# Block sums of the input spread over three feature tiles, and the first head's decay rows and context loaded before its query matrix

## The chip, the cores and the metric

One core of a Trainium2 chip runs the whole block. The metric is the device time of one execution, in microseconds (us). Engines are named as the profile names them: PE is TensorE's matmul, PEld its weight load, DVE is VectorE, ACT is ScalarE, POOL is GpSimd, and SP is SyncE, whose queue issues every DMA of this kernel.

## The reference

Two layers act on 1024 latent tokens of 1024 features, with a context of 256 tokens before them. Layer 0 mixes with a bidirectional mLSTM, layer 1 with box means over a grid of tokens. The part that matters here is layer 0:

```python
def mlstm_features(h, w_in, conv_w, conv_b, w_q, w_k, w_v):
    xm, z, og = jnp.split(h @ w_in, 3, axis=-1)
    xc = jax.nn.silu(short_conv(xm, conv_w, conv_b))
    q = headwise(xc, w_q)
    k = headwise(xc, w_k) * (MLSTM_HEAD_DIM ** -0.5)
    v = headwise(xm, w_v)
    return q, k, v, xc, z, og
...
        d = jnp.where(tril, b[..., :, None] - b[..., None, :] + ic[..., None, :], -jnp.inf)
        s = jnp.einsum("bhld,bhsd->bhls", qc, kc) * jnp.exp(d - m_t[..., None])
```

`h` is the input after RMSNorm and the shift and scale of the conditioning. `h @ w_in` gives three parts of 2048 columns: xm, z and og. The scores of a head are products of queries and keys, times decays exp(d).

## The kernel before

Every fp32 matmul is made of three: an operand is split into a rounded part and the rest (ACT casts, DVE subtracts), and hi·hi, hi·lo and lo·hi are summed in PSUM (`mm3`, line 136).

The stages, in order of time. **Start** (0 to 75 us): norms and the conditioning. **Feature tiles** (75 to about 395 us): 16 tiles of 128 columns of xm, `features(n)`, each in three chunks of 512, 512 and 256 tokens. ACT copies a chunk out of PSUM twice (L373 plain, L375 cast), DVE takes the rest of the split (L376). Then come the convolution (ACT L378, DVE L379 and L380, ACT SiLU L381), the split of its result (L388, L389) and the writes to DRAM. Between the matmuls of tile n+1, PE works through `token_part(n)`: ten small products (PSUM tag `pb`), each 128 tokens of tile n's cast xm against a small matrix; ACT copies each to SBUF (L415), and after five of them DVE adds (L416) and ACT casts (L418). `pb` has two buffers, so the product number s+2 needs the copy of product s. PE's order in this stage is written out by hand; each engine works strictly in the order of its own list.

**z and og columns** (to about 704 us): a seven-product block scheme (`strassen`) needs sums of blocks of h. Those are made by `block_sums()` during the feature tiles, four times (k = 0 to 3): load two rows of h from DRAM (L519), four DVE sums (L522 to L525), and for each of four results an ACT cast (L529), a DVE subtraction (L530) and a write to DRAM (L531). It is a generator, and the loop over tiles advances it by a number of `yield`s per tile, from tile 2 on.

**Heads** (704 to 1228 us): for each of four heads and eight query tiles, scores (`score_chunk`, chunks 0 and 1 of the latent tokens, chunk 2 of the context), decays (`decay`, ACT Exp of rows that are broadcast from DRAM, L769 to L773), their product (DVE L755), weights, transposes and values. Ahead of the first head stand the loads of its keys `xh_d`, `xl_d` (`fetch_x`: L692 latent, L686 context), of the decay rows (`load_gates` L713, `load_ctx_gates` L706), the matrix A (`make_A`) and the first queries (`make_q`: PE, ACT cast L735, DVE L736). In this stage a scheduler orders the instructions of every engine, each before the run and for good. **Rest**: output product, layer 1.

Large tiles share 32 buffers of 4 KB per partition (tag `S4`); `hn` has 3 buffers of 2 KB. In the block scheme's last tile all 32 are in use, and loads for the first head are issued as PE sets them free.

Of the kernel before, what the change touches and what calls it, by code (L numbers as in the profile page):

```python
# [17 lines left out]
P = 128  # L18
# [3 lines left out]
TC = 256  # L22
# [29 lines left out]
def hybrid_block(ctx: ExitStack, tc: tile.TileContext, xT, ctxT, vecs, w_ada0, w_ada, w_blk, w_krow, blk_mask, w_gate, w_in, b_gate, w_out,  # L52
# [10 lines left out]
    def nm(s):  # L63
        uid[0] += 1
        return f"{s}_{uid[0]}"
# [11 lines left out]
    def tl(tag, shape, dt=F32):  # L77
        n = int(np.prod(shape[1:])) * 4
        assert n <= BYTES[tag], (tag, shape)
        pool = ph["pool"] if tag in PHASED else sb  # L80
        return pool.tile(list(shape), dt, tag=tag, bufs=BUFS[tag], name=nm(tag))
# [3 lines left out]
    def pt_(tag, shape=(P, 512)):  # L85
        return ps.tile(list(shape), F32, tag=tag, bufs=PBUFS[tag], name=nm(tag))
# [4 lines left out]
    def f(t):  # L91
        return t.bitcast(F32)

    def const1(shape, name, dt=F32):
        return ph["pool"].tile(list(shape), dt, name=name)
# [157 lines left out]
    h = {}  # L253
# [94 lines left out]
    def bilinear():  # L348
        wkr = tl("S4", [P, KE, 4, 4])
        nc.sync.dma_start(wkr, w_krow)  # L350
        G.tensor_tensor(wkr, wkr, wb[:, 0, :, None, :].to_broadcast([P, KE, 4, 4]), op=ALU.mult)
        V.tensor_reduce(amat, wkr, axis=AX.X, op=ALU.add)
        V.tensor_scalar(amat, amat, QSCALE, None, op0=ALU.mult)
# [157 lines left out]
    def block_sums():  # L511


        dsh = const1([P, 4, 1], "dsh")
        V.tensor_tensor(dsh, mod0[:, 4:8, 0, 0:1], mod0[:, 0:4, 0, 0:1], op=ALU.subtract)
        for k in range(4):
            t0, t1 = tl("S4", [P, T]), tl("S4", [P, T])
            for t, kk in ((t0, k), (t1, k + 4)):
                nc.sync.dma_start(t, h_d[kk])  # L519
            yield  # L520
            b11, b12, b21, b22 = t0[:, :512], t0[:, 512:], t1[:, :512], t1[:, 512:]
            V.scalar_tensor_tensor(b22, b22, dsh[:, k], b12, op0=ALU.add, op1=ALU.subtract)  # L522
            V.tensor_tensor(b12, b12, b11, op=ALU.subtract)
            V.scalar_tensor_tensor(b11, b22, mod0[:, k, 0, 0:1], b11, op0=ALU.add, op1=ALU.add)
            V.scalar_tensor_tensor(b21, b21, mod0[:, k + 4, 0, 0:1], b11, op0=ALU.add, op1=ALU.subtract)  # L525
            yield
            for j, x in ((2, b11), (3, b22), (1, b12), (4, b21)):
                t = tl("S4", [P, 2, 512], F32R)
                S.activation(t[:, 0], x, AF.Copy)  # L529
                V.tensor_tensor(t[:, 1], x, f(t[:, 0]), op=ALU.subtract)  # L530
                nc.sync.dma_start(t_d[j - 1, k], f(t))  # L531
                yield

    side, parts, sums = iter(()), [], block_sums()
    with ctx0:
        gate_weights()
        for n in range(KE):
            out = features(n, side)
            for _ in side:
                pass  # L540
            if n == 1:
                gacc.extend(pt_("pc") for _ in range(3))
            if n == 2:
                bilinear()
            if n >= 2:
                for _ in range(3 if n < 10 else 2):
                    next(sums, None)
            parts.append(token_part(n, *out))
            if n:
                side = chain(*parts)  # L550
                parts = []
# [129 lines left out]
    def fetch_x(hd, h, ci):  # L681
        for part, src in (("xh", xh_d), ("xl", xl_d)):
            ts = hd.setdefault(part, {})
            if ci == 2:
                t = tl("S4", [P, 4, TC], F32R)
                nc.sync.dma_start(f(t), src[4 * h:4 * h + 4, :, T:TA].rearrange("c p t -> p c t"))  # L686
                for c in range(4):
                    ts[c, ci] = t[:, c]
                continue
            for c2 in range(2):  # L690
                t = tl("S4", [P, 2, 512], F32R)
                nc.sync.dma_start(f(t), src[4 * h + 2 * c2:4 * h + 2 * c2 + 2, :, 512 * ci:512 * ci + 512].rearrange("c p t -> p c t"))  # L692
                for j in range(2):
                    ts[2 * c2 + j, ci] = t[:, j]

    def fetch_v(hd, h, j0, j1):
        for j in range(j0, j1):
            for part, src in (("vh", vh_d), ("vl", vl_d)):
                t = tl("S4", [P, 2, DH], F32R)
                nc.sync.dma_start(f(t), src[h, :, 2 * j:2 * j + 2])  # L700
                hd.setdefault(part, []).append(t)

    def load_ctx_gates(h):
        rc = tl("hn", [P, 2, TC])
        for d in range(2):
            nc.sync.dma_start(rc[:, d], a_d[32 * d + h:32 * d + h + 1, T:TA].to_broadcast([P, TC]))  # L706
        return rc

    def load_gates(h):
        out = []  # L710
        for d in range(2):
            r = tl("S4", [P, T])
            nc.sync.dma_start(r, a_d[32 * d + h:32 * d + h + 1, 0:T].to_broadcast([P, T]))  # L713
            out.append(r)
        return out

    def make_A(h):
        ah, al = tl("wh", [P, 4, 32, 4], F32R), tl("wl", [P, 4, 32, 4], F32R)
        r = tl("wr", [P, 4, 32, 4])
        for c in range(4):  # L720
            V.tensor_tensor(r[:, c], mask, amat[:, 4 * h + c:4 * h + c + 1].to_broadcast([P, 32, 4]), op=ALU.mult)
        V.tensor_copy(ah, r)
        V.tensor_tensor(al, r, f(ah), op=ALU.subtract)
        return ah.rearrange("p c a b -> p c (a b)"), al.rearrange("p c a b -> p c (a b)")
# [113 lines left out]
    def start_head(h):  # L838
        hd = {}
        fetch_x(hd, h, 0)  # L840
        return dict(h=h, hd=hd)

    def next_q(cur, tp):
        return make_q(cur["hd"], cur["A"], tp)

    def finish_x(cur):
        for ci in (1, 2):
            fetch_x(cur["hd"], cur["h"], ci)

    cur = start_head(0)  # L850
    fetch_x(cur["hd"], 0, 1)
    cur["A"] = make_A(0)
    cur["q"] = next_q(cur, 0)
    cur["R"], cur["rc"] = load_gates(0), load_ctx_gates(0)
    fetch_x(cur["hd"], 0, 2)
    fetch_v(cur["hd"], 0, 0, 5)
    st_prev = st_now = nxt = None
    for i in range(len(seq) + 1):
        st = None
        if i < len(seq):  # L860
            h, ti = seq[i]
            more = h + 1 < NH
            st = dict(cur, ti=ti)
            decay(st)
            if ti == 7 and more:
                nxt["rc"], nxt["R"] = load_ctx_gates(h + 1), load_gates(h + 1)
            score_chunk(st, 0)
# [33 lines left out]
        if st and ti == 7:  # L901
            cur = nxt
# [385 lines left out]
```

## Time and profile before

| what | value |
|---|---|
| median of three runs | 2068.04 us (2063.6 to 2069.58) |
| profiled execution, its own time | 2062.41 us |
| its span | 2060.7 us |
| PE busy | 1982.7 us, 96% |
| DVE, ACT, POOL busy | 61%, 39%, 14% |
| mean granted clock of TensorE | 0.986 |
| HBM traffic | 164 GB/s over the span |

The span runs from the first to the last instruction of the profiled execution; its own time is 1.7 us longer. PE is busy nearly throughout: 78 us of the span have no matmul. The chain of waits is 86% PE.

### The profile page before, as it was taken

Reading aid. Unit: us, or ns where it says so; the run is one execution under the profiler, and the core shown is the slowest. Engines: PE = TensorE matmul, PEld = TensorE weight load, DVE = VectorE, ACT = ScalarE, POOL = GpSimd, SP = SyncE. Lnnn points to the kernel's source line nnn. Section 1 sums busy time; section 2 is a strip of 40 time slices with the busy share of each in tenths; the row PEclk is TensorE's granted clock in tenths of the full one; section 3 lists DMA queues with packets and bytes.
Section 4 is the critical chain, followed back from the end, with each engine's and each line's share of the span. In section 5 each row is a group of like instructions: output and inputs, shape, how many; then the busy total and the mean of one; then the engine's idle time right before and its main releaser. Section 6 shows DMA issues by size and latency. Waiting matters only on the chain.

```text
span 2060.7 us, 26787 instructions
## 1 busy us (share of the span) xinstructions
PE 1982.7 (96%) x10050; PEld 1668.4 (81%) x10050; DVE 1258.9 (61%) x2092; ACT 809.4 (39%) x1353; POOL 289.5 (14%) x376
## 2 busy tenths in 40 slices
PE   6888889999999999999999999999999999999997
PEld 4777778788888788888888878887888888888897
DVE  4766666787677667667576672544747283744444
ACT  5566666533333432333323322443423132224443
POOL 1000000023322100000000001343000000000275
PEclk9999999999999999999999999999999999999999
DMA  9376776864444854638346334534331312134573
GB/s 364 135 249 219 233 245 215 275 221 128 148 137 125 274 200 139 225 123 275 109 161 213 108 97 138 193 115 164 101 112 51 103 52 87 52 114 137 177 249 127
DMA packets 202499, 339.47 MB, mean 165 GB/s; under 512 B 13021, under 2 KB 116957, under 8 KB 202369
## 3 DMA queue, kind: packets, MB, share of 16 engines
q1 hardware_dynamic: 202368, 337.76, 48.8%
q8 instruction: 78, 1.28, 0.2%
q14 instruction: 53, 0.43, 0.1%
HBM read 234.77 MB, written 102.94 MB: 164 GB/s over the span
## 4 chain that ended last, share of the span: by engine, by line
PE 86%; DVE 5%; DMA 5%; ACT 2%; issue 1%; SPq 0%; POOL 0%; DVEq 0%; ACTq 0%; POOLq 0%
PE pa L136 43%; PE pc L136 34%; PE pb L136 7%; PE pb L796 1%; DMA wr<-in_w_ada_dram 1%; PE pc L827 1%; DMA S<-in_w_ada_dram 1%; DVE S L917 1%; DMA S<-in_ctxT_dram 0%; DMA vl_d<-T 0%; DVE wl L673 0%; DMA T<-in_bw_out_dram 0%; DMA S<-xh_d 0%; DMA cst<-in_w_blk_dram 0%; DVE wl L144 0%
## 5 line engine op out<-in xcount | busy, mean ns | idle before, releaser
L136 PE MATMUL pa<-S,wh 128*128 128x512 f32 (+1 forms) x2448 | 712.7, 376 | 1.7 <-ACT pt L375 1.7
L136 PEld LDWEIGHTS pa<-S,wh 128*128 128x128 f32 x2448 | 439.5, 191 | 72.2 <-ACT pt L375 2.9
L136 PE MATMUL pc<-S,wh 128*128 128x512 f32 (+1 forms) x1664 | 464.7, 365 | 3.2 <-ACT wh L142 2.3
L136 PE MATMUL pa<-S,wl 128*128 128x512 f32 (+1 forms) x1224 | 454.0, 371 | 3.3 <-DVE wl L144 3.3
L136 PEld LDWEIGHTS pc<-S,wh 128*128 128x128 f32 x1664 | 301.5, 189 | 54.6 <-ACT wh L142 2.5
L144 DVE TENSOR_TENSOR wl<-wr,wh 128x1024 fp32r<-128x1024 f32 (+1 forms) x124 | 146.9, 1185 | 267.2 <-ACT wh L142 266.0
L136 PE MATMUL pc<-S,wl 128*128 128x512 f32 (+1 forms) x832 | 302.3, 365 | 1.0 <-DVE wl L144 1.0
L136 PEld LDWEIGHTS pa<-S,wl 128*128 128x128 f32 x1224 | 233.1, 190 | 44.0 <-DVE wl L144 3.7
L142 ACT ACTIVATE wh<-wr 128x1024 fp32r<-128x1024 f32 (+1 forms) x124 | 124.6, 1005 | 358.1 <-PE pa L136 137.0
L136 PE MATMUL pa<-S,S 128*128 128x512 f32 (+1 forms) x1152 | 249.0, 362 | 5.4 <-DMA S<-xh_d 5.0
L136 PE MATMUL pc<-S,pt 128*128 128x512 f32 x960 | 227.5, 391 | 1.4 <-DVE S L736 0.9
L136 PEld LDWEIGHTS pa<-S,S 128*128 128x128 f32 x1152 | 191.7, 190 | 34.8 <-DMA S<-xh_d 5.5
L136 PEld LDWEIGHTS pc<-S,pt 128*128 128x128 f32 x960 | 178.2, 188 | 38.4 <-DVE S L736 1.6
L136 PEld LDWEIGHTS pc<-S,wl 128*128 128x128 f32 x832 | 157.5, 189 | 26.4 <-DVE wl L144 1.8
L798 ACT ACTIVATE pt<-pb 128x512 fp32r<-128x512 f32 (+1 forms) x96 | 47.8, 524 | 211.8 <-PE pb L796 202.7
L985 POOL TENSOR_TENSOR hn<-hn,pt 128x512 f32<-128x512 f32 (+1 forms) x48 | 77.7, 1621 | 308.4 <-ACT pt L984 307.4
L755 DVE SCALAR_TENSOR_TENSOR T<-pa,T 128x256 f32<-128x256 f32 (+3 forms) x184 | 78.1, 453 | 35.9 <-PE pa L136 31.4
L136 PEld LDWEIGHTS pb<-vv,S 128*128 128x128 f32 x256 | 48.3, 194 | 40.3 <-ACT S L375 16.2
L415 ACT ACTIVATE T<-pb 128x288 f32<-128x288 f32 x160 | 62.9, 412 | 43.2 <-PE pb L136 42.7
L585 ACT ACTIVATE wh<-T 128x512 fp32r<-128x512 f32 x70 | 41.2, 626 | 98.3 <-PE pc L136 79.6
L136 PE MATMUL pb<-S,wh 128*128 128x512 f32 x256 | 78.8, 389 | 0.0
L136 PE MATMUL pb<-vv,S 128*128 128x288 f32 (+1 forms) x256 | 50.1, 276 | 27.0 <-ACT S L375 14.5
(323 smaller groups left out, 2340.8 us busy)
## 6 DMA issues: line engine op xcount, KB each, us to landing
wr<-in_bw_in_dram SPq DMA_DIRECT2D x40, 512.0 KB, 3.5
wr<-in_w_in_dram SPq DMA_DIRECT2D x34, 512.0 KB, 4.3
wr<-in_w_ada_dram SPq DMA_DIRECT2D x32, 512.0 KB, 3.8
wr<-in_w_out_dram SPq DMA_DIRECT2D x32, 512.0 KB, 3.6
T<-in_bw_out_dram SPq DMA_DIRECT2D x32, 512.0 KB, 4.7
S<-y_d SPq DMA_DIRECT2D x28, 512.0 KB, 7.5
vh_d<-T SPq DMA_DIRECT2D x32, 320.0 KB, 2.8
vl_d<-T SPq DMA_DIRECT2D x32, 320.0 KB, 3.6
```

The lines of the kernel that those rows point to most:

```text
L136: PE.matmul(out, lhsT, rhs, start=start, stop=stop)
L142: S.activation(h, r, AF.Copy)
L144: V.tensor_tensor(l, r, f(h), op=ALU.subtract)
L415: S.activation(vst[:, :, s - s0], p, AF.Copy)
L585: S.activation(hi, a, AF.Copy)
L755: V.scalar_tensor_tensor(W[:, lo + sh:hi + sh], p[:, lo - o:hi - o], 1.0, W[:, lo + sh:hi + sh], op0=ALU.mult, op1=ALU.mult, accum_out=dp[ ...
L796: PE.transpose(p[:, j], st["M"][:, s * P:(s + 1) * P], ident)
L798: S.activation(th[:, :n], p[:, :n], AF.Copy)
L827: PE.transpose(p[:, c], hn[:, c * P:(c + 1) * P], ident)
L917: V.tensor_tensor(b, yraw[kp, hf], f(a), op=ALU.subtract)
L985: G.tensor_tensor(acc, acc, sq, op=ALU.add)
```

## The change

In `block_sums`, the pause between the loads and the sums goes, and of the four pauses after casts two stay. The loop now advances the generator once a tile: a tile with the loads and sums (tiles 2, 5, 8, 11), then one with two casts, then another with two. Ahead of the first head, the decay rows come second and the rest of the keys third, before A and the queries; the context's decay rows take a buffer of `S4` there.

```diff
@@ block_sums
                 nc.sync.dma_start(t, h_d[kk])
-            yield
             b11, b12, b21, b22 = t0[:, :512], t0[:, 512:], t1[:, :512], t1[:, 512:]
...
                 nc.sync.dma_start(t_d[j - 1, k], f(t))
-                yield
+                if j in (3, 4):
+                    yield
@@ loop over the feature tiles
             if n >= 2:
-                for _ in range(3 if n < 10 else 2):
-                    next(sums, None)
+                next(sums, None)
@@ load_ctx_gates
-        rc = tl("hn", [P, 2, TC])
+        rc = tl("hn" if h else "S4", [P, 2, TC])
@@ ahead of the first head
     cur = start_head(0)
-    fetch_x(cur["hd"], 0, 1)
+    cur["R"], cur["rc"] = load_gates(0), load_ctx_gates(0)
+    finish_x(cur)
     cur["A"] = make_A(0)
     cur["q"] = next_q(cur, 0)
-    cur["R"], cur["rc"] = load_gates(0), load_ctx_gates(0)
-    fetch_x(cur["hd"], 0, 2)
     fetch_v(cur["hd"], 0, 0, 5)
```

Below line 519 the changed kernel's line numbers are lower by one or two (L528 there is the cast L529 of before).

**ACT at the turn from tile 2 to tile 3, before.** S_181 is the cast of tile 2's xm (chunks 0 and 1), S_175 and S_206 to S_208 are the casts of block sums, S_173 and S_174 the summed rows, pb the token products.

```order
L418 ACTIVATE T_195_1131<-T_194_1130 128x640
L378 ACTIVATE T_202_1207<-T_179_1048,vec 128x1281
L529 ACTIVATE S_175_1038<-S_173_1030 128x512
L375 ACTIVATE S_181_1053<-pa_1055 128x512
L375 ACTIVATE S_181_1053<-pa_1103 128x512
L381 ACTIVATE T_202_1207<-T_202_1207 128x1281
L388 ACTIVATE S_204_1214<-T_202_1207 128x1024
L388 ACTIVATE pt_1213<-T_202_1207 128x256
L415 ACTIVATE T_219_1262<-pb_1270 128x2x144
L529 ACTIVATE S_206_1224<-S_174_1031 128x512
L529 ACTIVATE S_207_1228<-S_173_1030 128x512
L529 ACTIVATE S_208_1232<-S_174_1031 128x512
```

**The same engine after the change, from the middle of tile 2** (S_180 is there the cast of tile 2's xm):

```order
L373 ACTIVATE T_178_1044<-pa_1099 128x512
L415 ACTIVATE T_193_1126<-pb_1144 128x2x144
L375 ACTIVATE S_180_1049<-pa_1051 128x512
L375 ACTIVATE S_180_1049<-pa_1099 128x512
L415 ACTIVATE T_193_1126<-pb_1158 128x2x144
```

**and in tile 3**, where the first two casts now stand (pb_1306 is the fifth token product, pb_1324 the sixth; S_212 is tile 3's cast):

```order
L381 ACTIVATE T_201_1203<-T_201_1203 128x1281
L415 ACTIVATE T_217_1254<-pb_1296 128x2x144
L388 ACTIVATE S_203_1210<-T_201_1203 128x1024
L388 ACTIVATE pt_1209<-T_201_1203 128x256
L415 ACTIVATE T_217_1254<-pb_1306 128x2x144
L528 ACTIVATE S_205_1220<-S_173_1030 128x512
L528 ACTIVATE S_206_1224<-S_174_1031 128x512
L375 ACTIVATE S_212_1239<-pa_1241 128x512
L373 ACTIVATE T_210_1234<-pa_1289 128x512
L375 ACTIVATE S_212_1239<-pa_1289 128x512
L418 ACTIVATE T_218_1255<-T_217_1254 128x640
L415 ACTIVATE T_225_1316<-pb_1324 128x2x144
```

The cast of tile 2's xm moves from behind the first cast of a block sum to the middle of its own tile; two casts of sums stand in the tile after, ahead of the copy of the sixth token product.

**ACT ahead of the first head, before.** hn are results of the last og product (L616, Sigmoid), S_1060 the rounded queries, T_1048 and T_1079 decays.

```order
L616 ACTIVATE hn_6074<-pt_6072 128x512
L616 ACTIVATE hn_6097<-pt_6053 128x512
L616 ACTIVATE hn_6121<-pt_5995 128x512
L735 ACTIVATE S_1060_6158<-pc_6160 128x512
L735 ACTIVATE S_1060_6158<-pc_6169 128x512
L770 ACT_TABLE_LOAD
L770 ACTIVATE T_1048_6132<-S_1064_6178,cst_3885 128x128 x3
```

**The same place after the change** (S_1065 are the rounded queries; wh_6103 is the last weight split of the block scheme). First

```order
L584 ACTIVATE wh_6103<-T_1024_5973 128x512
L769 ACT_TABLE_LOAD
L769 ACTIVATE T_1048_6132<-S_1053_6141,cst_3885 128x128 x3
L771 ACTIVATE T_1079_6209<-S_1054_6143,cst_3885 128x1024
L768 ACTIVATE T_1085_6270<-S_1053_6141,cst_3885 128x128
L615 ACT_TABLE_LOAD
L615 ACTIVATE hn_6074<-pt_6072 128x512
L771 ACT_TABLE_LOAD
L771 ACTIVATE T_1085_6270<-S_1054_6143,cst_3885 128x896
```

then eight lines of further decays (ten instructions), and then

```order
L772 ACTIVATE T_1139_6575<-S_1055_6145,cst_3885 128x256
L615 ACT_TABLE_LOAD
L615 ACTIVATE hn_6097<-pt_6053 128x512
L615 ACTIVATE hn_6121<-pt_5995 128x512
L734 ACTIVATE S_1065_6169<-pc_6171 128x512
L734 ACTIVATE S_1065_6169<-pc_6180 128x512
```

The decays of four query tiles and four table loads now stand ahead of the cast of the first queries.

**SP ahead of the first head, after the change**: the decay rows (L712, L705) have the places that two key loads had, and the context keys (L685) stand ahead of the loads for layer 1's conditioning (L668) instead of behind them.

```order
L691 DMA S_1052_6139<-xl_d 128x2x512
L624 DMA gb_d<-S_1020_5965 128x4x128
L624 DMA gb_d<-S_1019_5964 128x4x128
L712 DMA S_1053_6141<-a_d 128x1024
L712 DMA S_1054_6143<-a_d 128x1024
L705 DMA S_1055_6145<-a_d 128x256 x2
```

Behind these stand four loads of latent keys, and then the two of the context keys.

## Rows read from the trace of the kernel before

**Rows 1.** The page's first line.
```profile
span 2060.7 us, 26787 instructions
```

**Rows 2.** Busy time by stretch: us, each engine's busy time, granted clock, DMA share, GB/s.
```profile
115.00:292.00 177.00, 153.64 (x790) 127.46 (x789) 115.98 (x182) 109.49 (x202) 2.28 (x28) 0.92 0.70 239
292.00:400.00 108.00, 107.07 (x591) 90.05 (x590) 74.72 (x112) 74.51 (x139) 1.92 (x14) 1.00 0.70 223
142.00:145.00 3.00, 2.66 (x7) 2.18 (x8) 3.00 (x6) 3.00 (x6) 0.00 (x0) 0.50 0.83 333
```

**Rows 3.** Waits of PE, 75 to 400 us: total, times, longest.
```profile
PE pb L136 <- ACT S L375: 14.5, 4, 4.0
PE pb L136 <- DVE S L376: 7.1, 4, 1.8
```

**Rows 4.** The chain in order of time, feature tiles: start, us, what.
```profile
159.51 2.75 PE pa L136 x12
292.10 2.75 PE pa L136 x12
362.18 2.75 PE pa L136 x12
```

**Rows 5.** Timeline, turn from tile 2 to 3: start, us, what, [idle before <-releaser].
```profile
138.99 0.63 ACT L529 ACTIVATE S<-S 128x512 fp32r<-128x512 f32 x1 [3.56 <-DVE S L524]
139.53 1.07 ACT L375 ACTIVATE S<-pa 128x512 fp32r<-128x512 f32 x2
140.16 0.40 PE L136 MATMUL pb<-vv,S 128*128 128x288 f32 x1 [3.63 <-ACT S L375]
142.34 0.49 PE L136 MATMUL pb<-vv,S 128*128 128x144 f32 x1 [1.78 <-DVE S L376]
```

**Rows 6.** Timeline of ACT and PE, a tile without block sums.
```profile
319.18 0.42 ACT L415 ACTIVATE T<-pb 128x288 f32<-128x288 f32 x1
322.37 0.59 ACT L373 ACTIVATE T<-pa 128x512 f32<-128x512 f32 x1
322.95 0.36 PE L136 MATMUL pb<-vv,S 128*128 128x288 f32 x2
```

**Rows 7.** Timeline, turn to the first head.
```profile
690.95 2.35 SPq L692 DMA_DIRECT2D S<-xh_d  x2
695.57 0.63 ACT L585 ACTIVATE wh<-T 128x512 fp32r<-128x512 f32 x1 [3.79 <-PE pc L136]
705.14 1.07 ACT L735 ACTIVATE S<-pc 128x512 fp32r<-128x512 f32 x2
705.83 3.87 PE L136 MATMUL pa<-S,S 128*128 128x512 f32 x16
706.23 1.28 ACT L770 ACT_TABLE_LOAD   x1
717.29 16.28 PE L136 MATMUL pa<-S,S 128*128 128x256 f32 x77 [5.04 <-DMA S<-xh_d]
```

**Rows 8.** ACT's groups, 710 to 723 us: line, shapes, count, busy us, mean ns.
```profile
L772 ACT ACTIVATE T<-S,cst 128x1024 f32<-128x1024 f32 (+3 forms) x4 | 3.9, 981 | 1.5 <-DMA S<-a_d 1.5
L773 ACT ACTIVATE T<-hn,cst 128x256 f32<-128x256 f32 x4 | 1.7, 509 | 0.0
L769 ACT ACTIVATE T<-S,cst 128x128 f32<-128x128 f32 (+2 forms) x3 | 1.5, 497 | 0.0
L771 ACT ACTIVATE T<-hn,cst 128x256 f32<-128x256 f32 x3 | 1.3, 502 | 0.0
L770 ACT ACTIVATE T<-S,cst 128x128 f32<-128x128 f32 x3 | 1.0, 392 | 3.8 <-DMA S<-a_d 3.8
```

**Rows 9.** DMA issues, 690.9 to 691.8 us: count, KB each, us to landing.
```profile
S<-xh_d SPq DMA_DIRECT2D x1, 512.0 KB, 7.5
```

**Rows 10.** Timeline of ACT, an earlier table load.
```profile
389.19 1.28 ACT L611 ACT_TABLE_LOAD   x1
390.48 0.60 ACT L611 ACTIVATE pt<-pa 128x512 f32<-128x512 f32 x1
```

## The prediction

> **What bounds the kernel now.** I read the span first [rows 1], then busy time and granted clock by stretch [rows 2], then who PE waits for in the worst stretch, then the chain in order of time and the timeline at its gaps.
>
> The stretches show where there is anything to gain. From 115 to 292 us PE is busy 153.6 of 177 us at a mean granted clock of 0.92; from 292 to 400 us, with the same feature tiles but no block sums, it is busy 107 of 108 at 1.00 [rows 2]. The loss belongs to four places: 14.5 us of waits for the cast of xm on ACT (L375) and 7.1 us for its rest on DVE (L376), four times each [rows 3].
>
> The timeline of the first shows the mechanism. ACT has the cast of a block sum (L529) in its list ahead of tile 2's L375, and stands idle for 3.56 us in front of it, until DVE's third sum is done. L375, whose input has long been in PSUM, runs only at 139.53; PE waits 3.63 us for it and 1.78 us more for L376 [rows 5]. Then the granted clock is 0.50, the lower of its two levels, in the 3 us from 142 [rows 2].
>
> What a stall costs in all is read from the chain, where each feature tile shows the same piece of 12 matmuls. From 159.51 to 292.10 are three pairs of tiles with a stall each, 132.59/3 = 44.20 us a pair; from 292.10 to 362.18 four tiles without, 70.08/4 = 17.52 us each [rows 4]. A stall costs 44.20 − 2·17.52 = **9.16 us**: 5.4 of idle PE, the rest mostly slower matmuls after it.
>
> The second place of the change is the turn to the first head: PE waits 5.04 us there, for the context keys [rows 7].
>
> **The change part by part.**
>
> *Block sums, the old stalls.* No work is added or removed: 16 sums, 16 casts, 16 subtractions, 8 loads and 16 writes. In the new order tile 2's two L375 stand in the middle of their own tile, between token copies, and no cast of a sum stands between a sum and them; the casts come a tile later, with all four sums long done. So the idle 3.56 us of ACT has no cause, and PE's wait with it. I take all four stalls as gone: −4·9.16 = **−36.6 us**. The first of the four lies ahead of the stretch that I averaged, but has the same two waits [rows 5].
>
> *Block sums, a new wait.* Two casts now stand in tile 3 (and 6, 9, 12) ahead of L375, L373, L375, L418 and the copy of the sixth token product; the eighth product needs the buffer that this copy frees. In a tile without sums the fifth copy ends at 319.6, chunk 1 comes out of PSUM from 322.37, and the eighth product starts at 322.95 [rows 6]. With the casts in place: 319.6, two casts of 0.6 [rows 5], one L375 of about 0.55, 321.4; then L373 has to wait for PE's chunk 1 as before, until 322.37. Behind it come L375, L418 and the copy, where in the old order the last two stood ahead of L373: 322.37 + 0.5 + 0.5 + 0.65 + 0.4 = 324.4 (the first three by L373's 0.59 less an overlap of 0.1 and with 640 columns for 512, the last as L415). So PE waits 324.4 − 322.95 = 1.5 us. In the second tile of casts (4, 7, 10, 13) the sixth copy stands ahead of L373, and there is no wait. That gives 4·1.5 = **+6.0 us**. Bounds: 0, if L373 is earlier than I think; above, a wait as long as today's, which also costs the clock, 4·9.16.
>
> *What else moves there.* DVE's sums stay at the turn of a tile, between L419 and the convolution, as today. They hold the convolution back by some 2 us, which the SiLU's place in ACT's list covers: the next copy behind it is due later. SP issues two writes of sums a tile instead of one and three, and the h loads still go ahead of the writes of v. Buffers: 20 of the 32 hold h, 8 hold xm and xc of two tiles, 2 the loaded rows, 2 the casts; the sums now keep their rows for two tiles more, and that just fits. All at 0, because the tiles without sums are set by PE alone.
>
> *Head start, the loads.* The decay rows are issued where two key loads stood, at 690.95 and the next place [rows 7]; a load issued there lands 7.5 us later [rows 9]. The context keys move ahead by about eight places in SP's list. PE's wait for them, 5.04 us, goes. Alone that would give −5 us.
>
> *Head start, ACT.* The list decides otherwise. Before, the first queries were rounded at 705.14, and scores began at 705.83, directly behind the block scheme [rows 7]. Now the decays of four query tiles, three sigmoids and four table loads stand ahead of that cast. ACT is free at 695.57 + 0.63 = 696.2 and loads a table until 697.5; the decay rows land at 690.95 + 7.5 = 698.45. The decays take 3.9 + 1.7 + 1.5 + 1.3 + 1.0 = 9.4 us [rows 8], about 8.8 with the overlap of neighbours. Three further table loads of 1.28 [rows 7] are 3.8, three sigmoids of 0.63 (the size of L585) 1.9, the first query cast 0.55. Sum: 698.45 + 8.8 + 3.8 + 1.9 + 0.55 = 713.5. PE is done with its query products at 705.83 and can do nothing without that cast, so it waits 7.7 us where it waited 5.04: **+2.7 us**. By 713.5 the context keys have landed too, and the decays are done, so I see nothing late next. The clock falls in both cases. Bounds: −5.0, if ACT is in time after all; +5, if the rows land 2 us later than I take.
>
> One rule of the skill weighs on the four table loads. The earlier load starts at 389.19, ends at 390.47, and the next activation starts at 390.48 [rows 10]: 1.28 us and nothing behind it. The Trainium skill ("ScalarE: Activation LUTs", section "What ACT_TABLE_LOAD costs") adds a drain of about 1.38 us to the load's 1.28 for every switch of table; an estimate by that page is 4·1.38 = 5.5 us more, +8.2 us at this place. The rows here show no such gap, so I keep 1.28.
>
> *Sum.* Against the profiled execution's own time, 1.7 us above its span: 2062.4 − 36.6 + 6.0 + 2.7 = 2034.5. The four executions shown (2062.4, 2063.6, 2068.0, 2069.6) have their middle at 2065.8, 3.4 above the profiled one, so I forecast 2034.5 + 3.4 = **2038 us**.
>
> **The rivals.**
>
> 1. *The head start pays too.* ACT is in time for the queries, and the 5.04 us come back: 2038 − 2.7 − 5.0 = 2030. For it speaks that the loads do move ahead; against it the list of ACT, which is fixed. 0.12.
> 2. *A table switch holds ACT for longer than its row.* Each load then also waits for the instruction ahead to leave the engine, and PE's wait at the head grows by 5.5 us: 2043. The gap of 0.01 us behind the load [rows 10] speaks against it. That is the skill's rule. 0.05.
> 3. *The new waits are long enough to cost the clock.* If the first cast tile stalls by 4 or 5 us instead of 1.5, each of the four costs about 5 instead of 1.5: 2038 + 14 = 2052. For it: DVE's part of the casts (L530) stands ahead of L376 as well, and h loads go ahead of the writes that free the tiles of v. Against: ACT's own walk above has only 1.5 us. 0.14.
> 4. *The wait only moves.* All 32 buffers are taken while sums and casts are held, so one late write of a cast keeps the next tile's xm out of its buffer, and PE waits for L375 as today, behind a DMA instead of a sum: about 2066, no change. Against it: in the new order tile 3's L375 has all its buffers' readers behind it. 0.08.
> 5. *Slower.* Casts now stand in eight tiles instead of four. If each pair stalls PE as one place does today, 8·9.16 = 73.3 us stand against 36.6, and the time is 2038 − 6 + 73 = 2105. It decides from (36.6 − 2.7)/8 = 4.2 us a tile on. Speaking for it: casts do stand ahead of L375 in all eight. Against: their sums are done a tile earlier. 0.06.
>
> **How the numbers follow.** The forecast has 0.55, with a range of its own of 2030 to 2046. A difference of 0.3%, 6 us, is about what a measurement of this kernel tells from no change. Faster are the forecast and rivals 1 to 3: 0.86; the same is rival 4, 0.08; slower is rival 5, 0.06. The range from 2025 (all stalls gone, no new wait, rival 1) to 2056 (rival 3 with a few us of spread) leaves out rivals 4 and 5 and a little of the others.
>
> **What would show each step right or wrong.** In the profile after: the waits of PE for L375 and L376 in the feature tiles, 21.6 us now, near zero; ACT's L528 with no wait for a DVE sum; the granted clock near 1.00 from 115 us on, and all tiles at 17.5 to 19 us. PE's waits for L415, if my 1.5 us are right, up by about 6 us, at four places. At the head: no wait for the context keys, and one wait of PE of 7 to 8 us for L734, with four table loads more on ACT. The prediction is wrong if waits for L375 return behind a DMA, if the clock still falls in tiles 3, 6, 9 and 12, or if the queries are cast near 706 us less what the features gave.

## The result, and the profile after

| | before | changed | ratio |
|---|---|---|---|
| median, four runs each | 2068.61 us (2063.6 to 2069.58) | 2037.37 us (2035.35 to 2039.99) | 0.9854, 95% interval 0.9833 to 0.9876 |
| profiled execution, its own time | 2062.41 us | 2039.13 us | |

The change makes the kernel 31 us faster by the medians (forecast: 2038), 23.3 us between the two profiled executions. The later experiments were measured beside fresh executions of the kernel before, whose medians are 2064.2 to 2064.9; so they are compared by their ratio to it.

Busy time by stretch, changed kernel (columns as in [rows 2], which these answer):

```profile
115.00:292.00 177.00, 173.22 (x959) 147.03 (x958) 130.25 (x204) 126.59 (x237) 2.45 (x31) 1.00 0.79 258
292.00:400.00 108.00, 104.24 (x568) 86.07 (x567) 83.71 (x123) 65.41 (x122) 6.81 (x14) 1.00 0.84 287
142.00:145.00 3.00, 3.00 (x17) 2.54 (x16) 1.08 (x3) 2.79 (x5) 0.00 (x0) 1.00 0.26 100
```

PE is busy 173.2 of 177 us where it was busy 153.6, and the granted clock stays at its upper level. Who PE waits for, 75 to 400 us and then 640 to 760 us (total, times, longest), against [rows 3] and the last row of [rows 7]:

```profile
PE pb L136 <- ACT T L415: 11.7, 9, 2.4
...
PE pa L136 <- ACT S L734: 7.5, 1, 7.5
PE pc L136 <- DVE wl L722: 1.1, 1, 1.1
```

No wait for L375 or L376 is left, and none for context keys. L415 had 6.3 us in five waits before; four have come, 5.4 us in all. ACT's own wait for the sums, in the kernel before (same columns), has no successor in the changed kernel:

```profile
ACT S L529 <- DVE S L524: 14.2, 4, 3.9
```

The chain's markers (start, us, what; as [rows 4]) give the tiles; the last row is for the last section:

```profile
134.93 2.76 PE pa L136 x12
153.84 2.75 PE pa L136 x12
171.37 2.76 PE pa L136 x12
188.87 2.75 PE pa L136 x12
207.81 2.76 PE pa L136 x12
...
1420.42 5.16 PE pc L136 x12
```

18.91 us for a tile with first casts, then 17.53, 17.50, and 18.94 again. A group of three is 1.4 us longer than three plain tiles. The timeline shows the first such place, the turn to the first head, and a row for the last section:

```profile
131.34 0.42 DVE L352 TENSOR_REDUCE amat<-S 128x64 f32<-128x256 f32 x1 [0.54 <-POOL S L351]
131.67 0.68 DVE L376 TENSOR_TENSOR S<-T,S 128x512 fp32r<-128x512 f32 x1
136.49 0.75 DVE L521 SCALAR_TENSOR_TENSOR S<-S,dsh,S 128x512 f32<-128x512 f32 x1
142.09 0.75 DVE L524 SCALAR_TENSOR_TENSOR S<-S,mod,S 128x512 f32<-128x512 f32 x1
145.22 1.15 ACT L528 ACTIVATE S<-S 128x512 fp32r<-128x512 f32 x2
146.27 0.59 ACT L375 ACTIVATE S<-pa 128x512 fp32r<-128x512 f32 x1
147.49 0.60 ACT L373 ACTIVATE T<-pa 128x512 f32<-128x512 f32 x1 [0.63 <-PE pa L136]
149.55 0.46 PE L136 MATMUL pb<-vv,S 128*128 128x288 f32 x2 [1.14 <-ACT T L415]
361.12 1.28 ACT L610 ACT_TABLE_LOAD   x1
...
665.71 1.28 ACT L769 ACT_TABLE_LOAD   x1
669.01 0.99 ACT L769 ACTIVATE T<-S,cst 128x128 f32<-128x128 f32 x3 [2.02 <-DMA S<-a_d]
671.77 1.28 ACT L615 ACT_TABLE_LOAD   x1
673.06 0.63 ACT L615 ACTIVATE hn<-pt 128x512 f32<-128x512 f32 x1
681.31 1.28 ACT L615 ACT_TABLE_LOAD   x1
683.66 1.55 ACT L734 ACTIVATE S<-pc 128x512 fp32r<-128x512 f32 x3
684.29 8.91 PE L136 MATMUL pa<-S,S 128*128 128x512 f32 x36 [7.45 <-ACT S L734]
...
1403.95 14.55 POOL L983 TENSOR_TENSOR hn<-hn,pt 128x512 f32<-128x512 f32 x7 [10.20 <-ACT pt L982]
```

The rest of xm (L376, at 131.67) now stands ahead of the sums; in [rows 5] PE waited for it behind them. One thing was not expected: DVE's sums (136.49 to 142.84) are over only 2.4 us ahead of the first cast, and stand among the steps of the convolution, as before the change. On the chip they are not a tile ahead.

To place gains and losses, each profiled execution is cut at instructions that all kernels have: L352's start on DVE, the first table load behind it at the end of the feature tiles (before: 129.49 and 389.19; the rows above: 131.34 and 361.12), the first query product, the first and the last transpose of a head's result (L826, L827), and the end.

| us | feature tiles | z and og | turn | heads | rest |
|---|---|---|---|---|---|
| before | 259.7 | 314.5 | 48.6 | 475.9 | 832.5 |
| changed | 229.8 | 312.0 | 50.3 | 476.7 | 837.1 |
| e1 sums only | 230.5 | 312.0 | 51.3 | 476.8 | 835.4 |
| e2 head only | 259.0 | 312.9 | 50.9 | 478.5 | 832.8 |
| e3 keys first | 229.2 | 312.9 | 48.1 | 477.4 | 832.1 |
| e4 keys, then rows | 229.5 | 312.0 | 50.6 | 479.2 | 832.8 |
| e5 four casts | 234.2 | 312.8 | 51.9 | 476.1 | 832.3 |
| e6 not ahead | 230.0 | 312.0 | 50.3 | 476.0 | 832.1 |
| e7 casts on POOL | 229.0 | 312.1 | 51.0 | 477.4 | 833.7 |
| e8 e3 and e7 | 228.9 | 312.1 | 47.2 | 480.5 | 832.7 |
| e9 sums on POOL | 236.8 | 312.8 | 52.0 | 476.3 | 832.3 |
| e10 casts elsewhere | 235.3 | 312.7 | 49.7 | 477.0 | 832.8 |
| e11 e3 and e9 | 238.3 | 312.8 | 46.9 | 480.0 | 832.4 |
| e12 e11, loads held | 236.8 | 312.8 | 48.6 | 478.1 | 832.5 |

Time ahead of L352, which no kernel changes, varies from 128.5 to 133.5 us.

### The profile page after: what moved, and what is told of

Same layout as the page of the kernel before. It is cut to its first block, busy times and chain, and to the rows that moved or that the text cites. A ratio compares the mean times of both kernels' runs of the same rounds, so it can differ in the third digit from the quotient of the medians.

```text
span 2037.3 us, 26773 instructions
## 1 busy us (share of the span) xinstructions
PE 1975.8 (97%) x10050; PEld 1665.4 (82%) x10050; DVE 1251.6 (61%) x2092; ACT 811.9 (40%) x1357; POOL 293.6 (14%) x376
## 4 chain that ended last, share of the span: by engine, by line
PE 84%; DVE 4%; ACT 3%; DMA 3%; POOL 3%; issue 2%; SPq 0%; DVEq 0%; POOLq 0%; ACTq 0%
PE pa L136 42%; PE pc L136 33%; PE pb L136 7%; PE pb L795 1%; POOL hn L983 1%; POOL S L1003 1%; DMA wr<-in_w_ada_dram 1%; DMA S<-h_d 1%; PE pc L826 1%; DVE S L915 0%; DVE wh L231 0%; DMA T<-in_bw_out_dram 0%; DMA S<-a_d 0%; DMA T<-in_w_ada_dram 0%; DVE T L754 0%
## 5 line engine op out<-in xcount | busy, mean ns | idle before, releaser
L136 PE MATMUL pa<-S,wh 128*128 128x512 f32 (+1 forms) x2448 | 704.6, 372 | 0.0
L136 PEld LDWEIGHTS pa<-S,wh 128*128 128x128 f32 x2448 | 434.4, 189 | 67.8
L144 DVE TENSOR_TENSOR wl<-wr,wh 128x1024 fp32r<-128x1024 f32 (+1 forms) x124 | 146.8, 1184 | 266.5 <-ACT wh L142 265.3
L415 ACT ACTIVATE T<-pb 128x288 f32<-128x288 f32 x160 | 62.3, 413 | 43.1 <-PE pb L136 35.2
L144 DVE TENSOR_TENSOR wl<-T,wh 128x1024 fp32r<-128x1024 f32 x32 | 45.5, 1422 | 46.2 <-ACT wh L142 46.2
L808 DVE BATCH_NORM_STATS2 st<-pc 128x6 f32<-128x512 f32 x32 | 22.4, 699 | 82.9 <-PE pc L136 82.9
```

Of the source, the lines that this page charges most:

```text
L136: PE.matmul(out, lhsT, rhs, start=start, stop=stop)
L144: V.tensor_tensor(l, r, f(h), op=ALU.subtract)
L415: S.activation(vst[:, :, s - s0], p, AF.Copy)
L808: V.bn_stats(b6, pv)
```

## The experiments

**The two parts apart.** e1 is the changed kernel with the old head start, e2 the old kernel with the new one:

```diff
@@ e1, against the changed kernel (e2: the reverse, in the kernel before)
     cur = start_head(0)
-    cur["R"], cur["rc"] = load_gates(0), load_ctx_gates(0)
-    finish_x(cur)
+    fetch_x(cur["hd"], 0, 1)
     cur["A"] = make_A(0)
     cur["q"] = next_q(cur, 0)
+    cur["R"], cur["rc"] = load_gates(0), load_ctx_gates(0)
+    fetch_x(cur["hd"], 0, 2)
```

> The changed kernel with the head start put back to its old order, so that only the block sums are changed. By the prediction's terms the head start costs 2.4 to 2.7 us, so this kernel is faster than the changed one: about 2035 us, with the wait of PE for the context keys (about 5 us) back and none of 7 us for L734. Rival: the head start pays by its earlier loads, and without it the time is about 2042 us. Third: the two turns cost the same, 2037 us.

> The kernel before with only the head start changed; the block sums stay in their four old places. By the prediction's terms it is slower than the kernel before by 2.4 to 2.7 us: about 2071 us, with the 21.6 us of waits for L375 and L376 unchanged and a wait of 7 to 8 us for L734 at the first head. Rival (the head start pays): about 2063 us.

Measured: e1 2036.82 us, ratio 0.9859 (0.9846 to 0.9872); e2 2065.22 us, ratio 1.0003 (0.9994 to 1.0011), that is +0.6 us (−1.2 to +2.3). All that can be measured comes from the sums; the head start is nearly free either way. The forecasts gave it 2.4 to 2.7 us, and e2's interval just leaves that out; what came is the third case of e1, two turns of equal cost. PE's waits at the turn, of e1 and of e2:

```profile
PE pa L136 <- DMA S<-xh_d: 6.4, 1, 6.4
```
```profile
PE pa L136 <- ACT S L735: 7.5, 1, 7.5
PE pc L136 <- DVE wl L723: 1.5, 1, 1.5
```

The new wait is there in e2 as forecast; but the old one is longer in e1's surroundings (6.4 us) than before (5.04).

**Other orders of the head start.** e3 puts the decay rows behind the queries again and keeps all keys ahead; e4 has latent keys, decay rows, context keys, queries.

```diff
@@ e3
-    cur["R"], cur["rc"] = load_gates(0), load_ctx_gates(0)
     finish_x(cur)
     cur["A"] = make_A(0)
     cur["q"] = next_q(cur, 0)
+    cur["R"], cur["rc"] = load_gates(0), load_ctx_gates(0)
@@ e4
+    fetch_x(cur["hd"], 0, 1)
     cur["R"], cur["rc"] = load_gates(0), load_ctx_gates(0)
-    finish_x(cur)
+    fetch_x(cur["hd"], 0, 2)
```

> The changed kernel, but the decay rows are loaded behind the queries again, as before; all keys of the first head, those of the context too, stay ahead. On ACT the cast of the first queries then stands directly behind the sigmoids, with no decay and no table load ahead. If the list of ACT is what makes PE wait at the head, the wait of 7.45 us for L734 goes; the decay rows are next to be late, since they are now behind the writes of the last gates and two loads for layer 1: they would land at about 686 us, PE can fill three buffers of scores until about 685, so a wait of 1 to 5 us for DVE's product with the decays takes its place: 2031 to 2035 us. Rival: the DMA queues are full at this turn (341 GB/s), any order of the same loads costs the same, and the time stays at 2037 us.

> The changed kernel with the loads of the first head in the order latent keys, decay rows, context keys, and then A and the queries. On ACT two of the sigmoids and the first query cast now stand behind three small decays only, and two table loads. If ACT's list sets the wait, the rows land at about 674.5 us, the query cast is done at about 678, and PE waits 1 to 2 us instead of 7.45: about 2031 us, and that is less than for the kernel with only the sums changed. Rival: the full DMA queues set the time of this turn, and the wait returns for the context keys: 2035 to 2037 us.

Measured: e3 2032.72 us, ratio 0.9844 (0.9831 to 0.9856); e4 2035.83 us, 0.9859 (0.9847 to 0.9872). In e3 the wait for L734 is gone and the forecast one stands in its place:

```profile
PE pa L136 <- DVE T L754: 4.8, 1, 4.8
```

e4 missed its 2031 us: PE waits 3.0 us for L734, less than half of the changed kernel's wait, yet the turn is as long as in the changed kernel. A second wait has come behind the first:

```profile
PE pb L795 <- DVE pt L798: 3.4, 1, 3.4
```

PE's busy time and granted clock behind the first (us, PE busy, clock, DMA share, GB/s):

```profile
676.00:680.00 4.00, 2.33 (x6) 0.62 1.07 382
680.00:684.00 4.00, 4.00 (x11) 0.53 1.06 398
684.00:688.00 4.00, 4.00 (x26) 1.00 1.06 409
```

The short wait still cost the clock: it is 0.62 and 0.53, near the lower of its two levels, in the two stretches from 676 to 684 us. Behind its longer wait the changed kernel has 0.65 from 680 to 684 us and 0.50 from 684 to 688.

**What removed the stalls.** e5 keeps the sums but has all four casts in one tile; e6 keeps the spread casts but has the sums, in the program, right ahead of them.

```diff
@@ e5
-                if j in (3, 4):
+                if j in (4,):
                     yield
...
-            if n >= 2:
+            if n >= 2 and n % 3 != 1:
                 next(sums, None)
@@ e6
                 nc.sync.dma_start(t, h_d[kk])
+            yield
             b11, b12, b21, b22 = t0[:, :512], t0[:, 512:], t1[:, :512], t1[:, 512:]
...
-            yield
             for j, x in ((2, b11), (3, b22), (1, b12), (4, b21)):
```

> The changed kernel with the sums still a tile ahead (tiles 2, 5, 8, 11), but all four casts in the one tile behind them (3, 6, 9, 12); the third tile of each group has none. If what counts is that the sums are done before their casts, the waits for L375 and L376 stay away, and only the wait for L415 in the cast tile grows, by what two more casts of 0.57 us add after the 0.63 us in which ACT now waits for PE: about 0.5 us in each of four tiles, 2039 us. If what counts is the spread of the casts over two tiles, the stalls come back: 8 to 9 us in each of four places, 2065 to 2070 us.

> The changed kernel with the casts spread over two tiles as in it, but the sums in the first of the two, directly ahead of their casts; the tile before has the loads alone. If the casts wait for sums that DVE has not done, ACT stands idle in front of L528 again, L375 is late, and the stalls of the kernel before return in tiles 3, 6, 9 and 12: 4 times (9.2 - 1.4) us more than the changed kernel, about 2068 us, with waits for L375 and L376. If the spread alone removed the stalls, the time stays at 2037 us.

Measured: e5 2041.48 us, ratio 0.9891 (0.9875 to 0.9908); e6 2038.03 us, 0.9870 (0.9855 to 0.9885). e5: no wait for L375, the L415 waits grow to 14.5 us, the tiles by 4.4 us instead of 2. So the spread is not what removed the stalls. e6 was a miss: no stall came back. Its only notable wait of PE, its last sum and its first casts are

```profile
PE pb L136 <- ACT T L415: 11.9, 9, 2.4
...
144.06 0.75 DVE L525 SCALAR_TENSOR_TENSOR S<-S,mod,S 128x512 f32<-128x512 f32 x1
147.19 1.15 ACT L528 ACTIVATE S<-S 128x512 fp32r<-128x512 f32 x2
```

The sums are over 2.4 us ahead of the casts, exactly as in the changed kernel: the edit moved them in the program, but not in DVE's list. So e6 does not test what the lead is worth. What e5 and e6 share with the changed kernel is the order in which buffers are taken. Before, the first cast of a sum takes its `S4` buffer in the pass that loads its rows, ahead of the xm of the pass behind it (S_175, then S_181, in the lists above). In the others that xm comes first (S_180, then the casts S_205 and S_206). e10 tests this in the old kernel, with sums, casts and pauses where they were.

```diff
@@ e10, against the kernel before
-                t = tl("S4", [P, 2, 512], F32R)
-                S.activation(t[:, 0], x, AF.Copy)
-                V.tensor_tensor(t[:, 1], x, f(t[:, 0]), op=ALU.subtract)
-                nc.sync.dma_start(t_d[j - 1, k], f(t))
+                t, lo = tl("pt", [P, 512], F32R), x.bitcast(F32R)
+                S.activation(t, x, AF.Copy)
+                V.tensor_tensor(lo, x, f(t), op=ALU.subtract)
+                nc.sync.dma_start(t_d[j - 1, k][:, 0], f(t))
+                nc.sync.dma_start(t_d[j - 1, k][:, 1], x)
```

> The kernel before, with its sums, casts and pauses in their old places and its old head start; only the casts' results no longer take buffers of S4: the rounded part goes to a buffer of pt, the rest is written over the sum, and both are written to DRAM apart. If the old stalls come from the buffer that the first cast takes ahead of the next tile's xm, so that L375 is put behind that cast, they go here: feature tiles of 229 to 232 us as in the changed kernel, instead of 259.7, and about 2037 us. Rival (the sums must stand a tile ahead of their casts, or the casts be spread over two tiles): the stalls stay, about 2064 us.

Measured: 2042.45 us, ratio 0.9893 (0.9878 to 0.9908). The waits for L375 and L376 are gone, and the feature tiles take 235.3 us: 24.4 of the 29.9 us come with this edit, which also splits the write of a result in two. Its timeline, at the place of [rows 5], and then a row of the kernel before:

```profile
132.33 1.10 ACT L375 ACTIVATE S<-pa 128x512 fp32r<-128x512 f32 x2
...
141.99 0.63 ACT L529 ACTIVATE pt<-S 128x512 fp32r<-128x512 f32 x1 [0.59 <-DVE S L524]
142.52 0.37 ACT L375 ACTIVATE pt<-pa 128x256 fp32r<-128x256 f32 x1
...
133.08 0.38 ACT L375 ACTIVATE pt<-pa 128x256 fp32r<-128x256 f32 x1
```

The cast L529 still waits for its sum, but L375 of the 1024 tokens now runs 9.7 us ahead of it. So the sum need not be done early for the stall to go. The 256-token cast, whose buffer is of `pt`, has gone the other way: it ran at 133.08, ahead of L529 (138.99 in [rows 5]), and now stands behind it. Either way the xm cast that shares its buffers with the cast of a sum is the one that stands behind it. What the last 5.5 us between e10 and the changed kernel (235.3 and 229.8) are is open. (The xm that waits in [rows 5] is that of the pass n = 3, one tile later than the prediction and the lists ahead of it call it; no number hangs on that.)

**Where the remaining 1.4 us a group come from.** e7 moves the casts to POOL, which is idle there.

```diff
-                S.activation(t[:, 0], x, AF.Copy)
+                G.tensor_copy(t[:, 0], x)
```

> The changed kernel with the sixteen casts of block sums moved from ACT to POOL, which is idle in the feature tiles. On ACT the token sums' cast L418 and the sixth copy then stand ahead of L373 in every tile, as in a tile without sums. If the order on ACT makes the 1.4 us of each first cast tile, the four waits for L415 go: 4 times 1.4 = 5.6 us less, about 2032 us. Rival: POOL's casts take 1.3 to 1.8 us each (its other operations of this size) and hold DVE back or the writes, and the time stays at 2037 us or gets longer.

Measured: 2033.0 us, ratio 0.9849 (0.9834 to 0.9863). The microseconds are near the forecast, but by the ratio to the kernel before it can't be told from the changed kernel (0.9854), and the reason failed. The first of the four waits is there unchanged, with no cast of a sum on ACT:

```profile
144.62 0.60 ACT L373 ACTIVATE T<-pa 128x512 f32<-128x512 f32 x1 [1.37 <-PE pa L136]
145.59 0.74 ACT L418 ACTIVATE T<-T 128x640 fp32r<-128x640 f32 x1
146.68 0.47 PE L136 MATMUL pb<-vv,S 128*128 128x288 f32 x2 [1.14 <-ACT T L415]
```

The four are 4.6 us instead of 5.4, and the feature tiles only 0.8 us shorter. The two casts are not what makes most of this wait. What is left is ACT's list: L418 and the sixth copy stand behind L373, with or without the casts. DVE's sums stand among the steps of the convolution just ahead of these places, so e9 takes the sums off DVE, and puts a whole tile more between them and their casts.

```diff
-            V.scalar_tensor_tensor(b22, b22, dsh[:, k], b12, op0=ALU.add, op1=ALU.subtract)
+            G.tensor_tensor(b22, b22, dsh[:, k].to_broadcast([P, 512]), op=ALU.add)
+            G.tensor_tensor(b22, b22, b12, op=ALU.subtract)
... the other three sums likewise: seven operations on POOL
             yield
+            yield
```

> The changed kernel with the sums of blocks on POOL, as seven plain additions and subtractions each time instead of DVE's four operations, and a whole tile between the sums and their first casts; the last two casts of a group go into the tile of the next loads. Moving the casts off ACT had left the wait for L415 in the first cast tile as it was, 1.14 us. So the theory now is that it comes from DVE: its four sums, 2.9 us, stand among the steps of the convolution and hold back the SiLU and all that stands behind it on ACT. Then the four waits go here: feature tiles from the bilinear reduction to the first table load behind them 224 us instead of 229.8, time about 2032 us. Rival: POOL's seven operations of 1.3 to 1.8 us hold DVE back or come too late for the casts, and the time stays at 2037 us or is longer.

Measured: 2044.87 us, ratio 0.9911 (0.9896 to 0.9926). The rival held. ACT's list in this tile did become that of a plain one, with L418 and the sixth copy (pb_1319) ahead of L373:

```
L375 ACTIVATE S_210_1234<-pa_1236 128x512
L418 ACTIVATE T_216_1250<-T_215_1249 128x640
L415 ACTIVATE T_223_1311<-pb_1319 128x2x144
L373 ACTIVATE T_208_1229<-pa_1284 128x512
```

But PE waits longer, since DVE's steps ahead of L418 and POOL's sums are all slower:

```profile
139.50 2.29 POOL L526 TENSOR_TENSOR S<-S,mod 128x512 f32<-128x512 f32 x1
141.75 2.55 POOL L522 TENSOR_TENSOR S<-S,S 128x512 f32<-128x512 f32 x1
146.03 2.10 DVE L389 TENSOR_TENSOR S<-T,S 128x1024 fp32r<-128x1024 f32 x1 [2.89 <-ACT S L388]
149.24 1.98 DVE L416 TENSOR_TENSOR T<-T 128x720 f32<-128x720 f32 x1
151.25 0.74 ACT L418 ACTIVATE T<-T 128x640 fp32r<-128x640 f32 x1 [4.16 <-DVE T L416]
152.34 0.47 PE L136 MATMUL pb<-vv,S 128*128 128x288 f32 x2 [2.38 <-ACT T L415]
```

**Gains put together.** e8 is e3 with e7, e11 is e3 with e9, and e12 is e11 with the loads L820 and L668 held back:

```diff
@@ e12, behind the first queries
+    late = cur["q"][1]
+    for tag, n in (("ab", 3), ("wr", 2)):
+        for _ in range(n):
+            G.tensor_copy(tl(tag, [P, 1]), f(late)[:, 0, 0:1])
```

> The casts of block sums on POOL and the head start with keys first and decay rows behind the queries, both in the changed kernel. If the two gains lie in separate stages they add: 2032.7 - 5.6 = about 2027 us, below both kernels. If a wait in one stage hides the other: 2030 to 2033 us.

> The sums on POOL with a tile ahead of the casts, and the head start with all keys first and the decay rows behind the queries. If both gains stand and add: feature tiles 224 us, the turn to the first head 47 to 48 us instead of 50 to 51, in all about 2028 us. Rival: one of them is lost in the other's stage, 2032 us.

> As the kernel with the sums on POOL and the keys first, and the loads of the gates' rows (L820) and of the conditioning for layer 1 (L668) held until the first queries are there: five one-column copies on POOL write their buffers first. The decay rows are then issued some 3 us earlier, behind the writes of the last gates alone. If the wait of 4.8 us for the product with the decays comes from the 1.75 MB in front of the rows, it falls to 1 to 2 us: about 2025 us. Rival: the rows wait for the buffers that PE frees, or the DMA queues are full either way: 2028 us as without.

Measured: e8 2033.42 us, ratio 0.9846 (0.9832 to 0.9861); e11 2043.1 us, 0.9901 (0.9886 to 0.9916); e12 2043.63 us, 0.9903 (0.9886 to 0.9919). All three missed. e11 and e12 carry e9's loss. At the turn e12 has what was wanted: PE's wait for the decays falls from 4.8 us (e11) to 0.8; but others, which e11 does not have, come behind it, up to the first results:

```profile
PE pb L803 <- DVE mv L819: 2.2, 1, 2.2
PE pc L834 <- DVE hn L823: 1.9, 1, 1.9
PE pb L803 <- DVE pt L806: 1.6, 1, 1.6
PE pa L136 <- DVE T L762: 0.8, 1, 0.8
```

No version is faster than the changed kernel beyond doubt: e3, e7 and e8 have the lowest ratios (0.9844 to 0.9849), and their intervals overlap its own.

## Why the prediction was right, step by step

- **Old stalls, −36.6, and new waits, +6.0:** together −30.6, measured −29.9 in the feature tiles (259.7 to 229.8). The waits for L375 and L376 are gone, the clock is 1.00, a cast tile is 18.9 us. The size of the stall was right, and so was the mechanism on ACT: no cast that waits for its sum stands ahead of L375 any more. Only the words "with all four sums long done" say too much: the sums are done 2.4 us ahead of the casts. What the prediction does not have is why the list had L375 behind the cast. e10 shows that it takes a cast whose result has an `S4` buffer, as the xm's has. That the scheduler puts L375 behind because its buffer comes free later is my reading of it, and order and number of the buffers were not tried apart.
- **The new wait, 1.5 a place:** measured 1.14, 1.14, 1.50 and 1.67, 5.4 in all. ACT's walk, 324.4 against 322.95, was right as a sum and in its end: L373 waits for PE (0.63 us), and L418 and the sixth copy stand behind it. That the casts put them there was wrong: without the casts on ACT (e7) they still stand behind, and four times 1.14 to 1.16 us stay. With the sums on POOL and a tile more ahead of the casts the list has it the other way (e9); which of the two does it, and whether the wait would then go, was not shown, since POOL slowed DVE. The second cast tiles have no wait, as forecast.
- **What else moves there, 0:** the prediction lets the SiLU's place cover the 2 us by which the sums hold the convolution back, and puts the sums between L419 and the convolution, where DVE has them among its steps. This zero is the doubtful one: if the sums on DVE turn ACT's list, it is what makes 4.6 of the 5.4 us, those that stay in e7. That is argued, not shown.
- **Head start, +2.7:** PE's wait was forecast at 7.7 us and is 7.45, and four more table loads stand on ACT. Two misses hide in it: the decay rows landed 8.6 us after their issue, not 7.5, and PE was done 1.1 us later, by a wait for L722 that the forecast does not have. The term itself was over-sized: +0.6 us (−1.2 to +2.3) by e2. It counted only PE's wait. From the first query product to the last transpose (turn and heads) the old head start has 524.5, 528.1 and 526.7 us (before, e1, e10), the new one 526.3 to 529.4 (changed, e2, e5, e6, e7, e9): 1.5 us between the means, with executions of one order 3 to 4 us apart.
- **"Nothing late next":** right for the changed kernel. For better orders it is wrong: in e3, e8 and e11 the turn is shorter by 2 to 4 us, and the heads longer by 1 to 4.
- **The sum:** 2034.5 for the profiled execution, measured 2039.1, so 4.6 too low. Of this, 1.9 lie ahead of L352, and 4.6 in the rest, where e3 to e12 are within 1.2 us of before; the z and og columns give 2.5 back, and features, turn and heads together add the remainder. No part of the change works ahead of L352 or in the rest. The step from the profiled execution to the median was taken as +3.4 and is −1.8 for the changed kernel, so 5.2 too high. The two errors cancel: that 2038 lies 0.6 us from the measured 2037.4 is luck, while the gain of the sums was foreseen.

**The rivals.** Rival 1 (2030) fell: ACT was not in time. Rival 2 fell: the load at 671.77 ends at 673.05, the next activation starts at 673.06. The drain of 1.38 us per switch, of which the Trainium skill tells ("ScalarE: Activation LUTs", section "What ACT_TABLE_LOAD costs"), is not seen in any of these loads. With it (an estimate by that page, 3 · 1.38 = 4.1 us more, since behind the first load ACT waits 2.02 us for rows anyway) PE's wait would have been 11.6 us, not 7.45. Rival 3 fell: the clock stays at 1.00. Rival 4, that a wait moves to a buffer, fell as worded; but the 32 buffers of which it speaks have a part in the old stall, by e10. Rival 5 fell: the eight cast tiles cost 4 · 1.4 us.

## What to carry to other kernels

When a scheduler orders the engines, ask what resource a result takes, not only when its input is ready: here an early buffer for work that wasn't urgent put urgent work behind it, on an engine that both share. A sum of stalls read from the chain gave the gain without the reason for the order, so test the reason by undoing one condition at a time (lead, spread, buffer) before building on it. And read the trace of such a test: e6 was made to take the lead away, and on the chip it did not. A wait taken away at a turn is no gain until the next stage has been read to its end.

## What was not expected of the hardware

**POOL and DVE slow each other.** With sums on POOL (e9), DVE's L389 takes 2.10 us instead of 1.23 and L416 1.98 instead of 0.90, and two of POOL's additions 2.29 and 2.55 us, where others of that group take 1.3. All of them read two inputs from SBUF. The Trainium skill ("SBUF — State Buffer", section "Who interferes with whom") says that a DVE instruction with two SBUF inputs contends with a GpSimd instruction that reads SBUF. The rows agree: where they overlap, each of these is longer by 0.9 to 1.3 us. Which engine held up the other they don't show.

**The same contention falls out two ways in one program.** In layer 1, POOL's seven additions of squares take 14.55 us in the changed kernel and 12.64 us in e3, DVE's seven additions beside them (L1003) 4.30 and 6.50 us. In the first case PE then waits 3.6 us for POOL's result, in the second 3.3 us for DVE's L144, some way ahead. Behind either wait the clock falls: to 0.56 from 1420 to 1426 us in the changed kernel, to 0.66 from 1409 to 1414 in e3. So the 12 matmuls at 1420.42 take 5.16 us, where e3, whose clock is back by then, has 2.87 for the same piece. e1 goes the way of the changed kernel (14.57 us). From these row statistics (L949) to the next ones, 504.1 us in all other executions, the changed kernel takes 506.4 and e1 506.0. So 2 us of a profile can come from which engine was first. That the order of arrival decides it is argued from these rows, not tried.
